# Two-layer hybrid attention kernel: product of a tile's first seven heads one step ahead in the last head of layer 1, four PSUM pairs in the projections of layer 0

## The chip, the cores and the metric

The kernel runs on one NeuronCore of a Trainium2 chip. The metric is device time in microseconds; lower is better. Engines are written as in the profile: PE (TensorE, matmuls), DVE (VectorE), ACT (ScalarE), POOL (GpSimd), SP (its queue issues most DMAs). PSUM, into which PE writes, has 8 banks of 128 x 512 float32; a "pair" here is two banks used as one 128 x 1024 tile.

## The reference

Two layers over 1024 latent tokens of width 1024 and 256 context tokens. Layer 0 is multi-head latent attention (16 heads), layer 1 differential attention (8 heads of two maps each). Each is gated by SiLU, multiplied by the output weights, added to the scaled residual and layer-normalised.

```python
def mla_mixer(h, h_c, rows, need_ctx, w_in, g_qa, w_qb, g_kva, w_kvb):   # layer 0
    q_lat, kv_lat, k_pe, gate = jnp.split(t @ w_in, splits, axis=-1)
    q = (rms_norm(q_lat, g_qa) @ w_qb).reshape(bsz, n, A_HEADS, A_NOPE + A_ROPE)
    kv = (rms_norm(kv_lat, g_kva) @ w_kvb).reshape(bsz, n, A_HEADS, A_NOPE + A_V)
...
    o, o_c = prefix_attention(q, k, v, q_c, k_c, v_c, (A_NOPE + A_ROPE) ** -0.5, need_ctx)
...
def diff_mixer(...):                                                      # layer 1
    q, k, v, gate = jnp.split(t @ w_in, 4, axis=-1)
...
    def combine(o1, o2, gate):
        o = o1 - lam_full.astype(o1.dtype) * o2
        o = rms_norm(o, g_sub) * (1.0 - lambda_init)
        return gated(o, gate)
...
        x = layer_norm(DEEPNORM_ALPHA * x + gate[:, None, :] * (o @ out_w[i]), ln_g[i], ln_b[i])
```

## The kernel before

Tokens are worked on in tiles of 128. A product of float32 accuracy is three matmuls (`mm3`, lines 184 to 187): both operands are split into a high and a low part, and low times low is left out. PE issues in the order of the program text (`manual_schedule`); in the projections at the start of layer 0's attention DVE does too. The other engines' orders are made by a scheduler at build time, which takes what it thinks ready, earlier text first. A PSUM pool (`set_banks`) has so many slots per tag; a new tile takes any slot of its tag that is free, and PE waits if none is.

**Layer 0's start (lines 613 to 883).** The pool has three pairs (tag a) and two single banks (tag d, for the products with V). The list at line 881 orders the work: `pq` and `pq2` make Q and its rotary part, `pk` makes K, each `vg` is one token tile of V (six matmuls of 512 columns into a pair), each `pm` is a piece of the row maxima of head 0 (`max0`: four tiles, the context columns with the maximum `ng`, then its transposition and the write of the maxima into four rows of `qH`). After it come the scores of head 0 (line 833). A V tile is scaled to float16 by ACT (line 650); its low part is made by ACT and POOL for even tiles (lines 653, 654), by DVE for odd ones (line 656). `ab1_of` and `h1_range` (lines 537 to 565) work out a bound for layer 1's input; they run beside head 0.

**The seam between the layers (lines 1145 to 1188).** Layer 0's output product of the tiles 0 to 7 goes by halves, y0 in a bank of tag a, y1 in the one bank of tag b. Then the pool becomes eight single banks of tag b, one is taken and dropped (line 1181), and the first product of layer 1, `made[0]`, starts; after it tile 7 is transposed (`z_turn`), for which its normalisation must be done.

**Layer 1's last head (lines 1569 to 1636).** Layer 1 goes head by head, and in a head tile by tile: a step (`step1`) for a tile t is

- S, the scores (`scores1`): one bank for the context columns of both maps, then two banks for map 0 and two for map 1. DVE takes the maximum of each bank; after map 0's three it makes the bound, and ACT can take the exponentials, which release the banks.
- V, the values (`values1`) of tile t-2, 30 matmuls into one bank; they follow S at once where the budget `at[0]` is 0, as it is in the last head (`SLOTO`).
- T, the transposes (`turn1`) of tile t-1's probabilities, in three pieces, and between them side work, dealt out by a budget of 7000 a slot.

In the last head (h = 7) the side work is the output product. A tile's attention of heads 0 to 6 is loaded (`out_load`), multiplied on POOL by its gate `g` (line 1479) and transposed (`out_turn`, line 1491); head 7 follows when V of the tile is done. `out_tile1(t)` then takes two banks, multiplies heads 0 to 6 for both halves, then head 7 (16 times three matmuls in all), adds the residual, and normalises. It runs in step t+2, so that the steps 0 and 1 have no side work and two steps (8 and 9) follow the last S. The last head's gate column is made at the end of head 6: ACT's SiLU (line 1327), a write to memory (line 1328), and from there `g` is read, two tiles at a time (lines 1458, 1478). Four of the eight blocks of output weights are split in `out_open` (lines 1464 to 1469), ahead of the last head.

Of the kernel before, what the change touches and what calls it, by code (L numbers as in the profile page):

```python
# [17 lines left out]
P = 128  # L18
# [35 lines left out]
def hybrid_kernel(  # L54
# [23 lines left out]
    def set_banks(**tags):  # L78
        pstack.close()
        banks.clear()  # L80
        banks.update(tags)
        banks["pool"] = pstack.enter_context(
            tc.tile_pool(name=nm("psum"), bufs=1, space=bass.MemoryType.PSUM, reuse_waits="tile"))
# [526 lines left out]
            pass  # L610
    p0.close()

    set_banks(a=3, d=2)
    a0 = ctx.enter_context(ExitStack())
    wk = a0.enter_context(spool("a0work"))
    Vh = wk.tile([P, NT, H0, V0 + 1], F16, name="Vh")
# [23 lines left out]
    def prod_v0():  # L640
        pool.memset(Vh[:, :, :, V0:V0 + 1], 1.0)
        for t in range(NT):
            ts = slice(t * P, (t + 1) * P)
            ps = pair()
            for hh in range(2):
                c = slice(hh * 512, hh * 512 + 512)
                mm3(ps[:, c], latH[:, 2, ts], latL[:, 2, ts], wv[0][:, c], wv[1][:, c], True, True)
            src = ps.rearrange("p (h d) -> p h d", d=V0)
            vh = Vh[:, t, :, :V0]
            act.activation(vh, src, AF.Copy, scale=vsc0)  # L650
            if t % 2 == 0:
                vf = w0("op").rearrange("p a b -> p (a b)")[:, :1024].rearrange("p (h d) -> p h d", d=V0)
                act.activation(vf, src, AF.Copy, scale=vsc0)
                pool.tensor_tensor(Vl[:, t, :, :], vf, vh, op=ALU.subtract)
            else:
                dve.scalar_tensor_tensor(Vl[:, t, :, :], src, vsc0, vh, op0=ALU.mult, op1=ALU.subtract)
            yield
# [221 lines left out]
    pm = max0(0, 0)  # L879
    with tc.manual_schedule(engines={ET.PE, ET.DVE}):  # L880
        for g in (pq, pk, pq, vg, pq, pq, vg, pk, pk, pq, pq1, vg, pq2, pq2, pq2, vg,
                  pm, vg, pm, vg, pm, vg, pm, vg, pm, vg, pm, vg):
            next(g)
    ow_ctx = ExitStack()

    def first(g, n):
# [18 lines left out]
    for h in range(H0):  # L905
        last = h == H0 - 1
        even, quad = (h + 1) % 2 == 0, (h + 1) % 4 == 0
        if h == H0 - 2:
            rp.close()
            ow = ow_ctx.enter_context(spool("o0w", side="right"))  # L910
            oH = ow.tile([P, KT, D], F32R, name="oH0")
            oL = ow.tile([P, KT, D], F32R, name="oL0")
            lw = load_outw(oH, oL, lambda: w0("ows"))
        if last:
            run_step(units0(h, 0) + units0(h, 2), [(max0(h, 2), (1, 0, 1)), (max0(h, 1), (0, 1, 1, 1, 2, 1)),
                                                   (lw, (1, 0, 1))])
            octx = {t: (w0(b_), w0(a_))[::-1] for t, a_, b_ in ((8, "rsw", "rr"), (9, "cs", "cs"))}

            def load_ctx():
                yield  # L920
                yield
                for t in (8, 9):
                    for x, d_ in zip(octx[t], (o_d[0], sg_d[0])):
                        sp.dma_start(x, d_[t * P:(t + 1) * P, :])
                    dve.tensor_tensor(*[octx[t][0]] * 2, octx[t][1], op=ALU.mult)
                yield

            run_step(units0(h, 1), [(load_ctx(), (1, 1, 1))])
            tv = lambda x: x.bitcast(F32R).rearrange("p (a b) -> p a b", a=KT)
            tctx = {8: (tv(w0("ows")), tv(w0("ows"))), 9: (tv(w0("rr")), tv(w0("cs")))}  # L930
            with tc.manual_schedule(engines={ENG[c] for c in MAN}):
                def turn_ctx(t):
                    tb = pair()
                    turn_out(octx[t][0], *tctx[t], [tb[:, :512], tb[:, 512:]])

                turn_ctx(8)
                retire(0)
                retire(1)
                for t in (8, 9):
                    y_ = pair()  # L940
                    yctx[t] = [y_[:, :512], y_[:, 512:] if t == 8 else bank("d")]
                    for hh in range(2):
                        c = slice(hh * 512, hh * 512 + 512)
                        mm_out(yctx[t][hh], *tctx[t], c)
                        if t == 8 and hh == 0:
                            turn_ctx(9)
                        flush()
        else:
            kq = chain(prod_k(h + 1), prod_q(h + 1, 0))
            low = [[(first(lw, 3), p_)] if h == H0 - 2 else [] for p_ in ((1, 0, 1, 0, 1), (1, 0, 1, 0, 1))]  # L950
            if h == 0:
                ab1_of()
            hr = [(h1_range(pair), (0, 1, 0, 1, 1))] if h == 0 else []
            run_step(units0(h, 0), hr + [(max0(h, 1), (1, 1, 2, 1, 1)), (max0(h, 2), (0, 1, 0, 1)),
                                    (kq, (2, 2, 1 + quad, 0, 0) if even else (2,))] + low[0])
            qs = chain(prod_q(h + 1, 1), prod_q(h + 1, 2))
            run_step(units0(h, 1) + units0(h, 2), [(max0(h + 1, 0), (1, 1, 1, 2, 1)),
                                                   (qs, (1, 1 + quad, 0, 1) if even else (2,))] + low[1])
# [16 lines left out]
    def w1(tag):  # L975
        sh, d, b = TAG1[tag]
        return rot(place[tag], sh, d, tag, b)
# [70 lines left out]
    with ow_ctx, spool("o0") as op0:  # L1048
# [94 lines left out]
        late = {0: (lam_,), 1: (lam_,), 2: (pw[0],), 3: (pw[0],), 4: (pw[0],), 6: (pw[1],), 7: (pw[1],)}  # L1143
        squares = {0: pw[0], 5: pw[1]}
        for t in range(8):
            y1, y0 = bank("b"), bank("a")
            mm_out(y0, *tHL[t], halves[0])
            if t:
                z_keep(t - 1)
# [28 lines left out]
                next(pw[1])  # L1178
        z_keep(7)
        set_banks(b=8)  # L1180
        bank("b")
        kcols, qcols = slice(P, 2 * P), slice(0, P)
        made = {0: [*proj1(512, 0, kcols)][-1]}
        z_turn(7, [bank("b"), bank("b")])
# [268 lines left out]
    def out_open():  # L1453

        prv.close()
        wg1 = a1.enter_context(spool("a1outg"))
        place["g"] = wg1
        TAG1["g"] = ([P, D], F32, 2)
        og["gb2"] = w1("wsq")
        bcast_row(og["gb2"], ln_g[1:2, :])  # L1460
        rest = [big.tile([P, 5, D], F32R, tag=tg, name=nm("o1")) for tg in ("bigA", "bigB")]
        oHL.extend([r[:, k - NOW, :] for r in rest] for k in range(NOW, KT))
        out_load(0)
        for k, w in enumerate(pre):
            if k % 2:
                split(*oHL[NOW + k], w, e_lo=pool)
            else:
                act.activation(oHL[NOW + k][0], w, AF.Copy, scale=gsub)
                dve.scalar_tensor_tensor(oHL[NOW + k][1], w, gsub, fv(oHL[NOW + k][0]), op0=ALU.mult, op1=ALU.subtract)
            if k == 0:  # L1470
                out_load(1)

    def out_load(t):

# [25 lines left out]
        out_turn(t, 4, 3)  # L1500
        yield 768

    def out_tile1(t):

        ts = slice(t * P, (t + 1) * P)
        tH, tL = oT[t]
        res = w1("res")
        sp.dma_start(res, zn_d[ts, :])
        y = [bank("b") for _ in range(2)]

        def mm(hh, k):
            c = slice(hh * 512, hh * 512 + 512)
            mm3(y[hh], tH[:, k, :], tL[:, k, :], oHL[k][0][:, c], oHL[k][1][:, c], k == 0, k == KT - 1)

        for hh in range(2):
            for k in range(KT - 1):
                mm(hh, k)
                yield 1600
                if hh == 1 and k == 3:
                    out_turn(t, KT - 1, 1)  # L1520
                    yield 256
        z, bs = w1("z"), w1("bs")
        for hh in range(2):
            mm(hh, KT - 1)
            c = slice(hh * 512, hh * 512 + 512)
            dve.tensor_tensor(z[:, c], y[hh], res[:, c], op=ALU.add)
            dve.bn_stats(bs[:, hh, :], z[:, c])
        yield 3200
        mv = w1("mv")
        dve.bn_aggr(mv[:, 0:2], bs)  # L1530
        rstd_of(mv[:, 2:3], mv[:, 1:2], 1.0, 1)
# [11 lines left out]
        pool.tensor_tensor(z, z, og["gb3"], op=ALU.add)  # L1543
        sp.dma_start(out[ts, :], z)
        yield 0

    credit = [0]

# [10 lines left out]
    with tc.manual_schedule(engines={ENG[c] for c in MAN1}):  # L1559
# [47 lines left out]
        for h in range(H1):  # L1607
# [9 lines left out]
            for t in range(SEQ // P):  # L1617
                if last:
                    if t >= 2:
                        out_load(t)  # L1620
                    G = weave(out_tile1(t - 2), out_turns(t - 1), (9, 12)) if t >= 2 else iter(())
                    if t == 2:
                        G = chain(out_turns(0), G)
                    credit[0] = 0
                step1((h, t), G, SLOT1 if not last else SLOTO)
                if last:
                    for _ in G:
                        pass
            for _ in G:
                pass  # L1630
        for t in range(SEQ // P - 2, SEQ // P):
            G = weave(out_tile1(t), out_turns(t + 1), (9, 12))
            credit[0] = 0
            step1(None, G, SLOTO)
            for _ in G:
                pass
# [74 lines left out]
```

## Time and profile before

| what | us |
|---|---|
| median of 3 runs (lowest, highest) | 1792.3 (1790.97, 1795.45) |
| the profiled execution's own time | 1792.78 |
| its span in the trace | 1790.9 |
| around the span | 1.88 |
| projections at the start of layer 0's attention | 223 to 259 of the span |
| seam of the layers (first product of layer 1) | 907 |
| last head of layer 1 | 1628 to 1791 |

Times in rows are counted from the start of the span. A timeline row has the start, the duration, the engine, the line of the kernel, the operation, output <- inputs, the shape, and in square brackets the idle time of the engine just before it and what ended it. A matmul's duration covers its run through the array; matmuls are issued closer together than that. A row of the windows has the busy time of each engine (with the number of instructions), then PE's mean granted clock as a share of full speed, then the share of DMA.

### The profile page before, as it was taken

The page shows a single profiled execution, that of the slowest core. Times are in us where ns is not written, and L with a number is a line of the kernel's source. Part 1 is how long each engine was busy: PE and PEld are TensorE (multiplying, and loading weights), DVE is VectorE, ACT ScalarE, POOL GpSimd, SP SyncE. Part 2 cuts the span into 40 slices and gives each one's busy share as a digit, 9 for nine tenths or more (in the row PEclk, how much of TensorE's full clock was granted, in tenths as well). Part 3 has the DMA queues.
Part 4 walks back from the last instruction along what each step waited for, and adds up shares of the span by engine and source line. Part 5 has one row for each costly group of instructions (what it writes and reads, how often), then busy time and mean ns, then how long its engine had stood idle before and what let it go on. Part 6 is the DMA issues. An engine that isn't in the chain of part 4 may idle for free. (4 is left out here: it accounts for less than half of the span.)

```text
span 1790.9 us, 36759 instructions
## 1 busy us (share of the span) xinstructions
PE 1664.6 (93%) x14564; PEld 1232.2 (69%) x14564; DVE 1228.9 (69%) x2045; ACT 1119.1 (62%) x2235; POOL 797.3 (45%) x724
## 2 busy tenths in 40 slices
PE   7999989999999998999999999999999999987998
PEld 6999955666666665577866666767675767566776
DVE  7658666575665666647855777777877787877664
ACT  2551167877777777845535676767676676757542
POOL 1432136767767776746551222231313131454454
PEclk9999999999999999999999999999999999998999
DMA  8358520110110122155532213131212122232331
GB/s 299 86 148 256 166 63 23 38 47 24 42 46 24 39 56 69 56 195 174 167 109 61 79 54 79 54 80 54 64 39 63 41 60 63 61 125 67 103 114 71
DMA packets 111226, 154.84 MB, mean 86 GB/s; under 512 B 13416, under 2 KB 84680, under 8 KB 111055
## 3 DMA queue, kind: packets, MB, share of 16 engines
q1 hardware_dynamic: 102654, 144.90, 27.2%
q10 hardware_dynamic: 8400, 7.61, 1.3%
q8 instruction: 114, 1.87, 0.5%
q14 instruction: 58, 0.47, 0.1%
HBM read 98.65 MB, written 27.07 MB: 70 GB/s over the span
## 5 line engine op out<-in xcount | busy, mean ns | idle before, releaser
L779 POOL TENSOR_TENSOR pl<-p,ph 128x1024 f16<-128x1024 f32 (+1 forms) x176 | 364.6, 2077 | 150.4 <-ACT ph L778 123.7
L1365 ACT ACTIVATE p<-ps_b,mx 128x512 f32<-128x512 f32 (+1 forms) x384 | 230.4, 617 | 85.0 <-DVE mx L1361 83.4
L777 ACT ACTIVATE p<-ps_a,esc 128x1024 f32<-128x1024 f32 (+1 forms) x176 | 189.0, 1074 | 94.5 <-PE ps_a L835 88.6
L759 DVE TENSOR_REDUCE mx<-ps_a 128x1 f32<-128x1024 f32 x128 | 155.2, 1222 | 128.3 <-PE ps_a L757 128.3
L778 ACT CAST ph<-p 128x1024 f16<-128x1024 f32 (+1 forms) x176 | 177.1, 1006 | 5.5
L1359 DVE TENSOR_REDUCE mx<-ps_b 128x1 f32<-128x512 f32 x256 | 165.5, 680 | 1.5 <-PE ps_b L1343 1.4
L848 PE MATMUL ps_d<-Vh,pl 128*128 128x65 f16 x1344 | 146.0, 194 | 4.5 <-POOL pl L779 4.4
L845 PE MATMUL ps_d<-Vh,ph 128*128 128x65 f16 x1344 | 148.1, 195 | 0.0
L847 PE MATMUL ps_d<-Vl,ph 128*128 128x64 f16 x1344 | 146.9, 193 | 0.0
L1342 PE MATMUL ps_b<-KS,QS 128*128 128x512 f16 (+1 forms) x384 | 127.9, 350 | 10.7 <-DVE pl L182 5.0
L845 PEld LDWEIGHTS <-ph 128*128 128x128 f16 x1344 | 123.2, 97 | 18.0 <-issue 4.6
L847 PEld LDWEIGHTS <-ph 128*128 128x128 f16 x1344 | 123.9, 98 | 12.1
L1378 PE MATMUL ps_b<-idr,p 128*128 128x128 f32 x640 | 103.4, 277 | 30.3 <-ACT p L1365 15.4
L1343 PE MATMUL ps_b<-KS,Q 128*128 128x512 f16 (+1 forms) x384 | 130.8, 349 | 0.0
L833 PE MATMUL ps_a<-qH,KH 100*128 100x512 f16 x320 | 121.8, 381 | 8.6 <-ACT p L777 4.2
L1390 POOL TENSOR_TENSOR sm<-sm,us 128x1 f32<-128x1 f32 x64 | 15.7, 246 | 255.0 <-DVE sm L1369 251.0
L848 PEld LDWEIGHTS <-pl 128*128 128x128 f16 x1344 | 123.1, 97 | 5.8 <-POOL pl L779 5.8
L182 DVE SCALAR_TENSOR_TENSOR pl<-ps_b,lcf,ph 128x512 f16<-128x512 f32 (+1 forms) x192 | 117.0, 654 | 13.0 <-ACT ph L181 13.0
L181 ACT ACTIVATE ph<-ps_b,lcf 128x512 f16<-128x512 f32 (+1 forms) x192 | 114.9, 646 | 17.0 <-PE ps_b L1378 17.0
L834 PE MATMUL ps_a<-qH,KL 96*128 96x512 f16 x320 | 121.6, 380 | 0.0
L835 PE MATMUL ps_a<-qL,KH 96*128 96x512 f16 x320 | 120.9, 378 | 0.0
L1378 PEld LDWEIGHTS ps_b<-idr,p 128*128 128x128 f32 x640 | 77.5, 142 | 56.5 <-ACT p L1365 23.7
(428 smaller groups left out, 5276.1 us busy)
## 6 DMA issues: line engine op xcount, KB each, us to landing
ws<-in_dw SPq DMA_DIRECT2D x28, 512.0 KB, 3.9
adw<-in_ada_w SPq DMA_DIRECT2D x24, 512.0 KB, 4.7
adaw<-in_ada_w SPq DMA_DIRECT2D x16, 512.0 KB, 7.7
g<-sg_d SPq DMA_DIRECT2D x16, 512.0 KB, 8.8
sg_d<-gg ACTq DMA_DIRECT2D x40, 128.0 KB, 3.7
o_d<-op SPq DMA_DIRECT2D x7, 640.0 KB, 4.0
xt<-in_xT SPq DMA_DIRECT2D x16, 256.0 KB, 3.8
wgs<-in_w_in SPq DMA_DIRECT2D x32, 128.0 KB, 3.1
```

Source lines behind the costliest of these rows:

```text
L759: dve.tensor_reduce(mx[:, t, 0:1], ps, axis=AX.X, op=ALU.max)
L777: act.activation(p32[:, :n], st, AF.Exp, scale=esc0)
L778: act.copy(ph[:, :n], p32[:, :n])
L779: pool.tensor_tensor(pl[:, :n], p32[:, :n], ph[:, :n], op=ALU.subtract)
L845: pe.matmul(pv[:, t, :], ph[:, ts], Vh[:, k, h, :], start=(k == kcs[0] and t == 0), stop=False, skip_group_check=True)
L847: pe.matmul(pv[:, t, :V0], ph[:, ts], Vl[:, k, h, :], start=False, stop=False, skip_group_check=True)
L848: pe.matmul(pv[:, t, :], pl[:, ts], Vh[:, k, h, :], start=False, stop=(k == NT - 1), skip_group_check=True)
L1342: pe.matmul(out, qs[m][:, ts], ks[m][:, c0:c0 + n], start=True, stop=False)
L1343: pe.matmul(out, q1[m][:, ts], ks[m][:, c0:c0 + n], start=False, stop=True)
L1359: dve.tensor_reduce(mx[:, 2 + 2 * m + i:3 + 2 * m + i], b, axis=AX.X, op=ALU.max, negate=True)
L1365: act.activation(p[m][:, c0:c0 + n], b, AF.Exp, bias=nb, accum_out=sm[:, 2 + 3 * m + i:3 + 3 * m + i])
L1378: pe.transpose(st[:, j * P:(j + 1) * P], pc[:, (k0 + j) * P:(k0 + j + 1) * P], idn)
```

## The change

In layer 0's start the pool has four pairs and no single banks; it goes back to three pairs and two banks after the list. Of the last six `pm` and `vg` the order is changed, and the V tiles whose low part goes by ACT and POOL are 1, 3, 5, 7 and 8 (still five of ten). `ab1_of` and `h1_range` run beside head 2. At the seam, tile 7's y1 goes into the bank of tag e, and no bank is dropped. In the last head of layer 1 the pool has five banks of tag b and three of a new tag y for the products; `g` has three buffers. A tile's heads 0 to 6 are multiplied one step earlier, in step t+1, of tile 0 half of them in step 0; head 7, the sum and the normalisation stay in step t+2. The splitting of the four weight blocks is dealt out over step 0.

```diff
-    set_banks(a=3, d=2)
+    set_banks(a=4)
...
-            if t % 2 == 0:
+            if t in (1, 3, 5, 7, 8):
...
-                  pm, vg, pm, vg, pm, vg, pm, vg, pm, vg, pm, vg):
+                  pm, vg, pm, vg, pm, vg, pm, pm, vg, vg, pm, vg):
             next(g)
+    set_banks(a=3, d=2)
...
-            if h == 0:
+            if h == 2:
                 ab1_of()
-            hr = [(h1_range(pair), (0, 1, 0, 1, 1))] if h == 0 else []
+            hr = [(h1_range(pair), (0, 1, 0, 1, 1))] if h == 2 else []
...
-            y1, y0 = bank("b"), bank("a")
+            y1, y0 = bank("b" if t < 7 else "e"), bank("a")
...
         set_banks(b=8)
-        bank("b")
...
-        TAG1["g"] = ([P, D], F32, 2)
+        TAG1["g"] = ([P, D], F32, 3)
...
+        set_banks(b=5, y=3)
         out_load(0)
+        out_load(1)
+
+    def out_split():
+
         for k, w in enumerate(pre):
...
-            if k == 0:
-                out_load(1)
+            yield 0
...
-    def out_tile1(t):
...
+    def out_mm(t, hh, k):
+
+        if k == 0:
+            oy[t, hh] = bank("y")
         tH, tL = oT[t]
...
+        c = slice(hh * 512, hh * 512 + 512)
+        mm3(oy[t, hh], tH[:, k, :], tL[:, k, :], oHL[k][0][:, c], oHL[k][1][:, c], k == 0, k == KT - 1)
+
+    def out_heads(t, hh, ks):
+        for k in ks:
+            out_mm(t, hh, k)
+            yield 1600
+
+    def out_last(t):
+
+        z, bs, res = w1("z"), w1("bs"), ores.pop(t)
+        for hh in range(2):
+            out_mm(t, hh, KT - 1)
             c = slice(hh * 512, hh * 512 + 512)
...
+            dve.tensor_tensor(z[:, c], oy[t, hh], res[:, c], op=ALU.add)
             dve.bn_stats(bs[:, hh, :], z[:, c])
         yield 3200
...
+    def out_step(s):
+
+        if s == 0:
+            yield from weave(chain(out_turns(0), *[out_heads(0, hh, range(NOW)) for hh in range(2)]), out_split(),
+                             (3, 5, 7, 9))
+            return
+        prev, opened = s - 2, s - 1
+        heads = range(NOW if s == 1 else 0, KT - 1)
+        if prev >= 0:
+            ores[prev] = w1("res")
+            sp.dma_start(ores[prev], zn_d[prev * P:(prev + 1) * P, :])
+        if opened < SEQ // P:
+            yield from out_heads(opened, 0, heads[:-2])
+        if prev >= 0:
+            out_turn(prev, KT - 1, 1)
+            yield 256
+        if opened < SEQ // P:
+            yield from out_heads(opened, 0, heads[-2:])
+        end = out_last(prev) if prev >= 0 else iter(())
+        yield from (v for _, v in zip(range(1), end))
+        yield from out_turns(s)
+        yield from end
+        if opened < SEQ // P:
+            yield from out_heads(opened, 1, heads)
...
-                    G = weave(out_tile1(t - 2), out_turns(t - 1), (9, 12)) if t >= 2 else iter(())
-                    if t == 2:
-                        G = chain(out_turns(0), G)
+                    G = out_step(t)
...
-        for t in range(SEQ // P - 2, SEQ // P):
-            G = weave(out_tile1(t), out_turns(t + 1), (9, 12))
+        for t in range(SEQ // P, SEQ // P + 2):
+            G = out_step(t)
```

More of the change, by code (lines that the diff above doesn't have):

```diff
@@ L1501, in out_turns @@
         yield 768
-    def out_tile1(t):
-        ts = slice(t * P, (t + 1) * P)
+    oy, ores = {}, {}
+    def out_mm(t, hh, k):
+        if k == 0:
+            oy[t, hh] = bank("y")
         tH, tL = oT[t]
[L1507 to L1511, printed above, removed]
-            c = slice(hh * 512, hh * 512 + 512)
[L1513 to L1526, printed above, removed]
+        c = slice(hh * 512, hh * 512 + 512)
[8 more added lines that the diff above has]
+            out_mm(t, hh, KT - 1)
+            c = slice(hh * 512, hh * 512 + 512)
+            dve.tensor_tensor(z[:, c], oy[t, hh], res[:, c], op=ALU.add)
             dve.bn_stats(bs[:, hh, :], z[:, c])
         yield 3200
+        ts = slice(t * P, (t + 1) * P)
         mv = w1("mv")
```

## The prediction

> **What bounds the kernel now.** First the span, then the last head's stretch by stages, then who PE waited for there. PE's last matmul starts at 1781.98 and issues in 0.23, so the stretch is cut at 1782.21; 1632.00 is the end of V of tile 6, head 6. Columns: bounds, length, busy time of PE, of its weight loads, DVE, ACT, POOL, PE's granted clock, DMA.
>
> ```profile
> span 1790.9 us, 36759 instructions
> 1632.00:1656.24 24.24, 14.70 (x114) 9.58 (x111) 20.07 (x33) 19.11 (x47) 14.38 (x13) 0.79 0.34 115
> 1656.24:1782.21 125.97, 125.85 (x781) 100.71 (x781) 75.25 (x152) 57.26 (x144) 60.17 (x63) 1.00 0.31 98
> PE ps_b L1378 <- DVE pl L182: 5.8, 1, 5.8
> PE ps_b L1378 <- DVE p L1371: 3.1, 1, 3.1
> 1686.74 0.28 PE L1342 MATMUL ps_b<-KS,QS 128*128 128x256 f16 x1
> 1691.34 0.40 PE L185 MATMUL ps_b<-oH,wx 128*128 128x512 f32 x1
> 1692.03 0.40 PE L185 MATMUL ps_b<-oH,wx 128*128 128x512 f32 x1
> 1703.70 0.28 PE L1342 MATMUL ps_b<-KS,QS 128*128 128x256 f16 x1
> 1704.04 0.27 PE L1343 MATMUL ps_b<-KS,Q 128*128 128x256 f16 x1
> 1705.87 0.22 PE L1386 MATMUL ps_b<-vh,ph 128*128 128x128 f16 x1
> 1781.98 0.39 PE L187 MATMUL ps_b<-o,wy 128*128 128x512 f32 x1
> ```
>
> From step 2's products on (1656.24) PE is the bound: 125.85 busy of 125.97 at full clock, a step each 16.96 (1703.70 - 1686.74). S takes 2.17 of it (to 1705.87), a head's three matmuls 0.69 (1692.03 - 1691.34). Only ahead of that is PE idle, 24.24 - 14.70 = 9.5, and it works there at a lowered clock. The first wait is for a bank: S of the last head held five of eight, V one, T two, and T's third piece waited 5.8 until DVE freed one. The second is for data.
>
> So filling the steps 0 and 1 can win no more than 9.5 and the lost clock. That is at most 0.21 x 24.24 = 5.1; in proportion to PE's work (14.70 of 24.24) I take 3.1. The work that PE has from 1632.00 to its end, at full clock, is then 150.2 - 9.5 - 3.1 = 137.6, and the change removes none of it.
>
> **The last head, step 0.** PE now meets tile 0's transposes right behind V of (6,6), and everything of PE stands behind them: T of (6,7), then step 1. They need tile 0 multiplied by a gate that comes out of the head before.
>
> ```profile
> 1628.47 1.17 ACT L1468 ACTIVATE o<-z,gsub 128x1024 fp32r<-128x1024 f32 x1
> 1632.54 1.15 ACT L1327 ACTIVATE gg<-gg,uw 128x1024 f32<-128x1024 f32 x1
> 1633.72 0.37 SPq L1328 DMA_DIRECT2D sg_d<-gg  x1
> 1637.50 0.85 SPq L1478 DMA_DIRECT2D g<-sg_d  x2
> 1642.14 4.12 POOL L1479 TENSOR_TENSOR ws<-ws,g 128x896 f32<-128x896 f32 x2 [1.81 <-DMA g<-sg_d]
> ```
>
> Here the gate is done at 1633.69, written from 1633.72, read from 1637.50, there at 1642.14, and tile 0 is multiplied by 1642.14 + 4.12/2 = 1644.2. The change takes the weight splitting (1.17 on ACT) out of the way, up to 1.1 earlier: 1643.1. SP no longer has a load of `res` ahead of the read, and fewer loads share the queues; if that halves the 3.8 between write and read, 1641.2, and 1640.3 with a quicker landing. I take 1641.8. Until then PE idles (V of (6,6) itself waits for one of five banks, inside this time).
>
> From 1641.8 the 137.6 follow, with four additions.
>
> **A bank for V in the steps 1 to 7.** S takes all five banks, and V, next in PE's order, needs the first that an exponential frees.
>
> ```profile
> 1620.09 0.68 DVE L1355 TENSOR_REDUCE mx<-ps_b 128x2 f32<-128x512 f32 x1
> 1622.32 0.69 ACT L1365 ACTIVATE p<-ps_b,mx 128x512 f32<-128x512 f32 x1 [3.19 <-DVE mx L1361]
> 1692.68 0.67 ACT L1365 ACTIVATE p<-ps_b,mx 128x512 f32<-128x512 f32 x1
> ```
>
> The context scores are in PSUM 0.61 after S begins (1704.04 + 0.27 - 1703.70); from DVE's first maximum to the end of the first exponential it is 2.92 (1620.09 to 1623.01), here with DVE and ACT waiting for nothing else. That is 3.53 against S's 2.17: a wait of 1.36, seven times, 9.5. The other end is the steady step of now, where ACT takes the previous tile's normalisation first and the first exponential ends at 1693.35, 6.61 after S began at 1686.74: 4.4 a step, 31 in all. The change moves that normalisation into the middle of the step, so I take the low figure; nothing below 0 is possible, and 0 is a rival.
>
> **The clock after idling, and the first split.** What idling costs is shown at the start of layer 0, and what a shorter wait costs beside head 0.
>
> ```profile
> 235.33 0.50 PE L185 MATMUL ps_a<-wvH,latH 128*128 128x512 f32 x1 [2.04 <-DVE stqL L182]
> 236.00:241.00 5.00, 4.73 (x21) 3.75 (x20) 2.33 (x4) 3.59 (x6) 1.20 (x1) 0.66 0.46 109
> 273.84 0.22 PE L768 MATMUL ps_a<-idr,ng 128*4 128x128 f32 x1 [1.44 <-DVE hm L300]
> 275.82 0.38 PE L833 MATMUL ps_a<-qH,KH 100*128 100x512 f16 x1 [1.38 <-DVE qH L769]
> 271.00:276.00 5.00, 2.17 (x31) 1.41 (x30) 4.57 (x18) 2.50 (x3) 3.67 (x2) 1.00 0.15 39
> ```
>
> After 2.04 of idling PE loses 0.34 x 5.0 = 1.7; waits of 1.44 and 1.38 in one stretch left it at 1.00. So step 0's wait costs 1.7 more, and the seven waits of 1.36 none. The transposes' copy to SBUF adds 0.6 (the row of ACT below).
>
> **The tail.** Before, V of tile 7 is followed by 42 matmuls of heads 0 to 6 that hide the way to head 7. After the change these stand ahead of V, and PE waits.
>
> ```profile
> 1771.01 0.22 PE L1388 MATMUL ps_b<-vh,pl 128*128 128x128 f16 x1
> 1771.88 0.19 ACT L1392 ACTIVATION_READ_ACCUMULATOR o<-o 128x1 f32 x1
> 1773.06 0.19 POOL L159 TENSOR_SCALAR ss<-ss 128x1 f32<-128x1 f32 x1
> 1773.92 0.35 DVE L1397 SCALAR_TENSOR_TENSOR ws<-o,ss,g 128x128 f32<-128x128 f32 x1 [2.22 <-POOL ss L160]
> 1778.65 0.27 PE L1491 MATMUL ps_b<-idr,ws 128*128 128x128 f32 x1
> 1778.96 0.27 ACT L176 CAST wx<-ps_b 128x128 fp32r<-128x128 f32 x1 [4.70 <-PE ps_b L1491]
> ```
>
> V to the accumulator's end 1.06 (1771.01 to 1772.07), POOL to the end of the scaling 1.21 (1773.06 to 1774.27), transpose to the end of its copy 0.58 (1778.65 to 1779.23): 2.9. The last six matmuls, 1.38 at full clock, then run at half, 1.3 more: 4.2. POOL's normalisation of tile 6 may stand in between: up to 6.
>
> Sum: 1641.8 + 137.6 + 9.5 + 1.7 + 0.6 + 4.2 = 1795.4 against 1782.2: the last head loses **13.2**. What follows the last matmul stays.
>
> **Layer 0's start.** PE takes 35.60 there, with these waits beside the 2.04 shown.
>
> ```profile
> 223.06:258.66 35.60, 28.70 (x121) 20.57 (x119) 23.24 (x22) 21.39 (x23) 12.34 (x7) 0.92 0.31 82
> PE ps_a L757 <- DVE Vl L656: 1.4, 2, 0.7
> PE ps_a L185 <- DVE mx L759: 1.1, 2, 0.5
> 256.25 0.22 PE L768 MATMUL ps_a<-idr,ng 128*4 128x128 f32 x1 [2.12 <-DVE ng L765]
> 231.03 3.06 DVE L295 TENSOR_TENSOR rr<-rr,rsw 128x1024 f32<-128x1024 f32 x1
> 230.93 2.07 POOL L654 TENSOR_TENSOR Vl<-op,Vh 128x1024 f16<-128x1024 f32 x1 [5.58 <-ACT op L653]
> ```
>
> All but the 2.12 are waits for a pair; a fourth covers them, and two V tiles (twelve matmuls of 0.23) now stand ahead of the transposition that waited 2.12. Waits together 6.7, lost clock 0.08 x 35.6 = 2.8: at most 9.5. DVE's sum of 3.06 ran beside POOL's subtraction and ended 1.1 after it; with tile 0 on DVE (its 1.28 of line 656 takes POOL's place) the two don't meet. DVE is busy 23.24 and ACT 21.39 of it whatever the pairs, and the loads of K and Q still come in their order, so I take two thirds, **-6.5**; 0 at worst, since no engine gets more work but DVE 1.28 early and less late.
>
> **Head 2 for head 0, the seam.** The 1.44 and 1.38 above are head 0's wait for the bound's small operations; beside head 2 they come in the same order ahead of the same `ng`: what one head wins the other loses, 0 (from -2 to +1).
>
> ```profile
> 907.15 0.38 PE L185 MATMUL ps_b<-h1H,wx 128*128 128x512 f16 x1 [2.00 <-DVE z L1083]
> 910.12 1.24 ACT L1092 ACTIVATE z<-z,mv 128x1024 f32<-128x1024 f32 x1 [5.88 <-POOL mv L1091]
> ```
>
> `made[0]` waits 2.00 for tile 7's y1 in its bank. With y1 elsewhere it starts at 905.15, and its 24 matmuls (S's 2.17 are eight of that width and four half as wide, so 0.217 each) end at 910.4; `z_turn` then waits for ACT until 911.36. So **-0.9**, between 0 and -2.
>
> **Sum.** The profiled execution took 1792.78 (1.88 around its span), 0.5 above the median: 1792.8 + 13.2 - 6.5 - 0.9 = 1798.6, **1799**.
>
> **The rivals.**
>
> *The bank is there in time* (not slower). If a bank frees within S's own 2.17 the steps lose nothing: 1798.6 - 9.5 = 1789; with all of layer 0's 9.5 won, 1786. It decides from the point where the first exponential ends before S does. Against it stands 2.92 in DVE and ACT alone; for it, that T's 5.8 shows the wait only with eight banks full.
>
> *The fill pays.* If tile 0 is ready by 1637, PE starts 4.8 earlier: 1794. For it: 1.1 of ACT and the `res` load go; against it: the landing took 4.64 (1637.50 to 1642.14) and the product 2.06.
>
> *The clock falls in each step.* The waits for a bank come once in some 18 us; if each cools the clock as 2.04 did, seven times 1.7: 1811. Against it the row with 1.44 at clock 1.00; for it, that DVE or ACT need be only 0.7 late for a wait of 2.04. (The Trainium skill, TensorE: Matmul & The Clock Gate, A second HAM failure mode: psum-queue depth-cycling, describes a kernel in which cycling through PSUM left PE idle so often for moments that its clock swung between half and full. By that rule this is the time; here the rows show it from 2.04 on and not at 1.44.)
>
> *The pairs don't bind.* If DVE and ACT set layer 0's start, nothing is won there: 1805.
>
> **How the numbers follow.** Forecast 0.46, bank in time 0.26, fill 0.11, clock 0.08, pairs 0.09. A measurement here tells 0.3% from no change, 5.4 us: faster is below 1786.9, slower above 1797.7. The forecast's own range is 1793 to 1805, about four fifths of it slower; clock and pairs are slower; the fill is mostly no change; the bank case is half faster, half no change. Slower 0.56, same 0.29, faster 0.15. The range 1786 to 1811 leaves out the far ends (31 for the banks, a last head that gains).
>
> **What would show it.** V's first matmul in each step waiting for ACT's exponential, 1.4 long, with S's period near 18.3; step 0 with a wait of PE at tile 0's transposes until about 1642; a gap of 3 in PE ahead of the last six matmuls; head 0's first scores at about 252 in place of 258.66; `made[0]` without its 2.00. It is wrong if the steps keep 16.96, or if PE's stretch from step 0 on begins well ahead of 1640.

## The result, and the profile after

The change makes the kernel slower: 1821.8 us (median of 4 runs, 1818.3 to 1825.7) against 1791.6 (4 runs, 1788.0 to 1795.5) beside it, a ratio of 1.0166 with a 95% interval of 1.0149 to 1.0184, so about 30 us. The forecast was 1799, with 1811 as the end of the range. The profiled execution of after took 1823.78, with 1821.9 of span.

First the last head of both kernels in one row each, from the first matmul of S of (7,0) to the end of the last matmul (columns as in the forecast's rows of windows). The first fence is before, the second after; after's two other rows start at tile 0's transposes and cover one steady step.

```profile
1628.14:1782.37 154.23, 144.57 (x936) 113.17 (x933) 99.34 (x190) 80.21 (x196) 75.95 (x78) 0.97 0.31 99
```

```profile
span 1821.9 us, 36757 instructions
1623.61:1813.40 189.79, 153.76 (x936) 121.17 (x933) 100.76 (x190) 80.65 (x196) 81.40 (x78) 0.93 0.24 80
1640.43:1813.65 173.22, 147.75 (x892) 116.91 (x892) 88.67 (x173) 66.51 (x169) 74.80 (x73) 0.94 0.21 72
1706.88:1727.10 20.22, 17.32 (x110) 13.55 (x109) 11.72 (x23) 7.55 (x22) 9.71 (x8) 1.00 0.31 101
```

PE issues the same 936 matmuls in both, and the stretch is 35.6 longer. PE's idle time in it goes from 9.7 (154.23 - 144.57) to 36.0, which is 26.4 of the 35.6; the other 9.2 is the same work done at a lower clock (0.93 in place of 0.97). A step takes 20.2 instead of 16.96. The last head began 4.5 earlier (1623.61 for 1628.14): 35.6 - 4.5 is the 31 by which the spans differ.

Next, what PE waited for in the last head of after (the view of waits: total, times, longest), and one steady step in order of time (the first matmul of S, DVE, ACT, then V).

```profile
PE ps_b L1386 <- ACT p L1365: 24.0, 8, 6.3
PE ps_b L1495 <- DVE ws L1397: 7.0, 6, 4.3
PE ps_b L1495 <- POOL ws L1483: 3.8, 1, 3.8
1706.88 0.28 PE L1342 MATMUL ps_b<-KS,QS 128*128 128x256 f16 x1
1707.53 0.69 DVE L1355 TENSOR_REDUCE mx<-ps_b 128x2 f32<-128x512 f32 x1 [2.21 <-PE ps_b L1343]
1708.14 2.48 DVE L1359 TENSOR_REDUCE mx<-ps_b 128x1 f32<-128x512 f32 x4
1710.53 0.45 DVE L1361 TENSOR_SCALAR mx<-mx 128x1 f32<-128x1 f32 x2
1710.83 0.69 ACT L1365 ACTIVATE p<-ps_b,mx 128x512 f32<-128x512 f32 x1 [3.73 <-DVE mx L1361]
1711.66 0.22 PE L1386 MATMUL ps_b<-vh,ph 128*128 128x128 f16 x1 [2.44 <-ACT p L1365]
```

The wait for V's bank is there, at the instruction and behind the engine that the forecast named, eight times (6.3 of it in step 0, 2.4 to 2.8 in the steps 1 to 7). What differs is DVE: it takes all four maxima of line 1359 in one go, map 1's two among them, and only then makes a bound. So the first exponential ends 4.64 after S begins (1711.52 - 1706.88), not 3.53.

The second row of waits is head 7's transposition, which waits for line 1397, the scaling that V's result goes through. The third is tile 0 in step 0: the way of the gate, from the SiLU to the first transposes.

```profile
1628.04 1.15 ACT L1327 ACTIVATE gg<-gg,uw 128x1024 f32<-128x1024 f32 x1
1629.21 0.37 SPq L1328 DMA_DIRECT2D sg_d<-gg  x1
1632.58 0.32 SPq L1560 DMA_DIRECT2D res<-zn_d  x1
1633.00 1.32 SPq L1482 DMA_DIRECT2D g<-sg_d  x3
1637.61 2.77 POOL L1483 TENSOR_TENSOR ws<-ws,g 128x896 f32<-128x896 f32 x1 [5.06 <-DMA g<-sg_d]
1640.43 1.75 PE L1495 MATMUL ps_b<-idr,ws 128*128 128x128 f32 x7 [3.75 <-POOL ws L1483]
```

Nothing on this way got shorter: 3.79 from the write's issue to the read's (3.78 before), 4.61 until the read has landed (4.64 before), a load of `res` still ahead of it on SP (line 1560, which the program text has only in step 2), and the gate itself as long after S began as before (5.58 and 5.55). The product on POOL even took longer: 2.77 where half of before's 4.12 is 2.06.

At the other places: the first scores of head 0 come at 251.29 (258.66 before), the two waits for the bound of layer 1's input now stand beside head 2, as long as they were (1.50 and 1.4 for 1.44 and 1.38), and `made[0]` starts without its wait.

### The profile page after: what moved, and what is told of

The parts are those of the page before. It is cut to its first block, busy times and chain, and to the rows that moved or that the text cites. A ratio compares the mean times of both kernels' runs of the same rounds, so it can differ in the third digit from the quotient of the medians.

```text
span 1821.9 us, 36757 instructions
## 1 busy us (share of the span) xinstructions
PE 1673.5 (92%) x14564; PEld 1239.2 (68%) x14564; DVE 1230.0 (68%) x2045; ACT 1120.0 (61%) x2235; POOL 802.4 (44%) x724
## 5 line engine op out<-in xcount | busy, mean ns | idle before, releaser
L1386 PE MATMUL ps_b<-vh,ph 128*128 128x128 f16 x640 | 115.6, 224 | 24.2 <-ACT p L1365 24.0
```

## The experiments

All runs are medians against the kernel before on the same chip. The last column is the last head from S of (7,0) to the end of the last matmul, from each trace.

| run | what | us | ratio (95%) | last head |
|---|---|---|---|---|
| before | | 1791.6 | 1 | 154.2 |
| after | | 1821.8 | 1.0166 (1.0149 to 1.0184) | 189.8 |
| E1 | layer 0 and seam alone | 1784.7 | 0.9953 (0.9939 to 0.9968) | 152.7 |
| E2 | last head alone | 1825.6 | 1.0187 (1.0171 to 1.0202) | 188.8 |
| E3 | after, V between the maps | 1797.9 | 1.0033 (1.0022 to 1.0045) | 165.8 |
| E4 | after, three heads between the maps | 1826.3 | 1.0186 (1.0170 to 1.0202) | 190.3 |
| E5 | E3, three heads kept for the tail | 1797.0 | 1.0042 (1.0029 to 1.0056) | 166.2 |
| E6 | E3, tile 0 a step later | 1796.3 | 1.0041 (1.0028 to 1.0054) | 163.7 |
| E7 | after, map 0's bound first | 1817.3 | 1.0146 (1.0129 to 1.0162) | 184.0 |
| E8 | before with banks 5 and 3 | 1830.6 | 1.0228 (1.0215 to 1.0241) | 194.3 |
| E9 | before with four pairs | 1791.4 | 1.0003 (0.9992 to 1.0013) | |
| E10 | E1, splits in step 1 | 1787.3 | 0.9980 (0.9970 to 0.9989) | 156.5 |
| E11 | E1, splits in step 0 | 1786.2 | 0.9973 (0.9962 to 0.9985) | 155.6 |
| E12 | E1 with banks 5 and 3, V between the maps | 1804.5 | 1.0071 (1.0054 to 1.0087) | 173.4 |

Profiled executions differ by some us ahead of the last head where the code is the same (it begins at 1619.20 in E3's and at 1625.97 in E6's), so lengths of that stretch are compared, not its place.

**E1 and E2: which half of the change.** E1 has the hunks of the diff for layer 0, for head 2 in place of head 0 and for the seam, with the old last head; E2 has the others, with the old layer 0 and seam.

> The layer 0 edits, head 2 for head 0 and the seam's bank, with the last head as it was before. Theory (the two parts of the change add, and the whole loss lies in the last head): the first scores of head 0 come at about 251.3, the last head starts 4.5 earlier than before (1623.6 for 1628.14) and takes 162.8 as before; time 1787. Rival (the gain of layer 0 is lost again further on, since the last head waits for loads and for the gate that do not move with it): 1790.5 to 1792.

> The last head's edit alone, layer 0 and the seam as before. Theory (the parts add): the last head takes 198 instead of 162.8, time 1791.6 + 30.2 + 4.5 = 1826. Rival (part of the loss comes from the earlier start, which only moves PE's work ahead of data that come when they came): at most 1822.

E1 gains 7.4 (1784.67 against 1792.08, the theory had 1787) and E2 loses 33.5 (1825.63 against 1792.08, as the theory had it). Together that is a loss of 26, against 30 for the whole change; by the intervals of the three ratios the two agree. E2 shows the same row of waits for V's bank, 24.0 in 8 waits, so nothing in it needs the earlier start. E1 is faster than both kernels, and no other version that was run has a lower median.

**E3: V between the maps.**

```diff
                 if cur:
                     S = scores1(*cur)
                     next(S)
             some(side, at[0])
             with tc.high_priority(HP):
+                if at is SLOTO and turned:
+                    values1(*turned.pop(0))
                 if cur:
                     next(S)
-                if turned:
+                if at is not SLOTO and turned:
                     values1(*turned.pop(0))
```

> The changed kernel with V put between the scores of map 0 and of map 1 in the last head, so that V needs no bank that an exponential frees; what waits for such a bank is then the fifth piece of S, behind 3.2 us of V. Theory (the wait for V's bank is what the steps lose, and the clock falls with it): the seven waits of 2.44 (17.7 in all) go and with them most of the clock lost in the steps 1, 2 and 6 (1.7 + 1.6 + 1.7); S's period goes from 20.2 to about 17.3; time 1799 to 1804. Step 0's 6.3 does not count, since tile 0 is awaited there anyway. Rival (the step is set by the way from scores over exponentials, T and its splits to V): PE waits elsewhere in the step as long, time 1815 to 1822.

The theory's step came true, and the time is a little below its 1799: 1797.9. The 3.2 for V in that text is V at about half clock; at full clock it takes 1.6. The profile of E3, waits and one step:

```profile
PE ps_b L1495 <- POOL ws L1483: 9.9, 1, 9.9
PE ps_b L1495 <- DVE ws L1397: 5.1, 2, 4.3
PE ps_b L1342 <- ACT o L1391: 2.2, 1, 2.2
1674.23:1691.42 17.19, 17.06 (x110) 13.61 (x110) 12.01 (x23) 9.22 (x23) 8.79 (x9) 1.00 0.35 120
```

V's row is gone, a step is 17.19 at full clock, and the last head is 24.0 shorter than in after. The waits left are step 0's for tile 0 (9.9; V of (6,6), which stood in this wait, is done earlier now) and the tail's 4.3.

**E4: the same cover, taken from behind V.**

```diff
-                step1((h, t), G, SLOT1 if not last else SLOTO)
+                step1((h, t), G, SLOT1 if not last else (4800 if t else 0, *SLOTO[1:]))
```

> The changed kernel with three heads' products of the open tile (nine matmuls, 2.07) put between the scores of map 0 and of map 1 in the steps 1 to 7. Theory (as for V between the maps): DVE has only map 0's maxima at hand, so its bound comes 1.2 earlier; the first exponential ends about 3.6 after S begins, V stands at 4.24: no wait, S's period about 17.3, time 1799 to 1804. Rival (the way from scores to T sets the step; map 1's scores now come 2.07 later, and so does everything behind them): 1810 to 1822, with PE waiting at T or at the next V for the splits.

Neither: V's wait all but goes, and the time doesn't fall. The waits of E4 (7.1 of the second row stands in step 0):

```profile
PE ps_b L1495 <- DVE ws L1397: 23.8, 7, 4.3
PE ps_b L1386 <- ACT p L1365: 9.8, 4, 7.1
```

The three heads' products that now stand ahead of V are missing behind it, where in after five heads' products covered the way from V over ACT, POOL and DVE to head 7's transposition. That wait was 7.0 in after; here it is 23.8, some 3.3 in each steady step (13.1 in four between 1680 and 1770). Work can cover one of two waits, and in after the second was only just covered.

**E5 and E6: what is left of E3.** E5 keeps three heads' products of tile 7 for the last step; E6 moves tile 0's transposes and its first products out of step 0.

```diff
+        if s == SEQ // P + 1:
+            yield from out_heads(prev, 1, range(KT - 4, KT - 1))
         if prev >= 0:
             out_turn(prev, KT - 1, 1)
...
-            yield from out_heads(opened, 1, heads)
+            yield from out_heads(opened, 1, range(KT - 4) if s == SEQ // P else heads)
```

```diff
-            yield from weave(chain(out_turns(0), *[out_heads(0, hh, range(NOW)) for hh in range(2)]), out_split(),
-                             (3, 5, 7, 9))
+            yield from out_split()
             return
...
-        heads = range(NOW if s == 1 else 0, KT - 1)
+        heads = range(KT - 1)
+        if s == 1:
+            yield from out_turns(0)
```

> V between the maps as in the run before, and of tile 7 the last three heads' products of the second half (nine matmuls, 2.07) kept for the last step, behind V of tile 7. Theory (the 4.3 of the tail is the uncovered way from V over ACT, POOL and DVE to head 7's transposition): that wait falls from 4.3 to about 2.3 and the last matmuls run at a higher clock; 1797.9 - 2.1 to - 3.4, so 1794.5 to 1796. Rival (the three heads are missed in step 8, where V of tile 7 then waits for T's splits): 1797 to 1799.

> V between the maps, and tile 0's transposes with its first four heads' products moved from step 0 to step 1, behind S of (7,1) and V of (6,7); the splits of the last weights stay in step 0. Theory (PE waits 9.9 at tile 0's transposes for the gate's way through DRAM, with everything behind them): T of (6,7), S and V of step 1 (2.2 + 3.2, T about 2) run inside that wait; the wait falls by 5 to 7.3, time 1790.6 to 1793. Rival (S of (7,1) has to wait for the banks that the exponentials of (7,0) free, and these come late in step 0): 1796 to 1798.

Both come out at the times of their rivals, and by the intervals neither differs from E3 in time. The rows of E5, then of E6:

```profile
PE ps_b L1495 <- DVE ws L1397: 3.7, 2, 2.9
PE ps_b L1386 <- ACT ph L181: 0.9, 1, 0.9
```

```profile
1636.62 0.58 PE L1342 MATMUL ps_b<-KS,QS 128*128 128x512 f16 x1 [5.98 <-ACT p L1365]
```

In E5 the tail's wait falls from 4.3 to 2.9 and V of tile 7 now waits 0.9 for T's split, as the rival said; the last head is no shorter (166.2 and 165.8). In E6 the 9.9 is gone, but the fifth piece of S of (7,0) itself waits 5.98 for a bank that an exponential of (7,0) holds; S of (7,1), which the rival named, starts behind that, at 1640.41, without such a wait. ACT starts that exponential only at 1635.79, behind the gate's SiLU and four casts of weights. So step 0 can't work ahead of its own exponentials with five banks, and the last head is only 2.1 shorter.

**E7: map 0's bound ahead of map 1's maxima.** The bound's instruction writes two columns more, which map 1's maxima overwrite, so DVE can't take those first.

```diff
+            if h == H1 - 1 and m == 0:
+                dve.tensor_scalar(mx[:, 4:7], mx[:, 0:3], mx[:, 3:4], mx[:, 0:1], op0=ALU.min, op1=ALU.min)
+            else:
-            dve.tensor_scalar(nb, mx[:, 2 * m + 2:2 * m + 3], mx[:, 2 * m + 3:2 * m + 4], mx[:, m:m + 1],
+                dve.tensor_scalar(nb, mx[:, 2 * m + 2:2 * m + 3], mx[:, 2 * m + 3:2 * m + 4], mx[:, m:m + 1],
```

> The changed kernel, but map 0's bound writes two more columns that map 1's maxima overwrite, so that DVE must take it ahead of them; the same number of instructions. Theory (the forecast's 1.36 was right for map 0's maxima alone, and the other 1.1 is map 1's two maxima of 0.6 taken ahead of the bound): V's wait falls from 2.44 to about 1.3 in each of seven steps, S's period from 20.2 to about 19.0; 1821.8 - 8 = 1814, and 1808 to 1810 if waits so short leave the clock at 1.00. Rival (the first exponential is held by ACT or by PE, not by DVE's order): 1820 to 1823.

The profile of E7 (its lines 1362, 1368 and 1389 are the bound, the exponential and V): one step, V's waits between 1660 and 1770, then the waits of the whole last head.

```profile
1706.33 1.28 DVE L1359 TENSOR_REDUCE mx<-ps_b 128x1 f32<-128x512 f32 x2
1707.65 0.32 DVE L1362 TENSOR_SCALAR mx<-mx 128x3 f32<-128x3 f32 x1
1708.00 0.69 ACT L1368 ACTIVATE p<-ps_b,mx 128x512 f32<-128x512 f32 x1 [2.49 <-DVE mx L1362]
PE ps_b L1389 <- ACT p L1368: 9.5, 6, 2.3
...
PE ps_b L1389 <- ACT p L1368: 18.0, 8, 6.3
PE ps_b L1498 <- DVE ws L1400: 8.1, 7, 4.3
```

The four maxima fall apart into two and two, and the exponential follows the first pair. The waits for V's bank lose 6.0 (24.0 to 18.0), the last head 5.8. Without the longest, which is step 2's, the waits between 1660 and 1770 are 1.4 each ((9.5 - 2.3) / 5), where the theory said 1.3; the steps 1 and 2 still wait 2.3. The median falls by 4.5 where the theory had 8 or more, and as the intervals of E7 and after overlap, it is the trace and not the time that shows the step. In the steps 3 to 7 DVE's order is the difference between 1.4 and 2.4 of wait.

**E8 and E12: the banks without the move.** E8 is the kernel before with `set_banks(b=5, y=3)` in the last head and `y` taken from the three; E12 is that on E1, with E3's order of V and the maps.

```diff
+        set_banks(b=5, y=3)
...
-        y = [bank("b") for _ in range(2)]
+        y = [bank("y") for _ in range(2)]
```

> The kernel before with five banks for S, V and T and three for the products in the last head, and nothing moved: layer 0 as before. Theory (the fewer banks make V wait for an exponential, whatever stands ahead; here ACT takes the previous tile's normalisation first, and the first exponential ends 6.61 after S begins against S's 2.17): V waits about 4.4 in each of the steps 1 to 7, the time rises by some 25 to 31, 1817 to 1823. Rival (the loss needs the moved products: with the old order DVE and ACT are relieved elsewhere and V waits no more than 1): 1792 to 1800.

> The layer 0 and seam edits (1784.7), the old last head's order with five banks for S, V and T and three for the products, and V put between the scores of map 0 and of map 1. Theory (five banks cost only through V's wait, and what the changed order still loses with V between, 1797.9 against 1784.7, lies in step 0's wait for tile 0 and in the tail, which the old order does not have): V's wait goes, the fifth piece of S waits at most about 1 a step because ACT takes the previous tile's normalisation ahead of the first exponential; 1785 to 1792. Rival (five banks cost also at T and at the fifth piece, whatever the order): 1797 or more, with S's period at 18.5 or above against 16.96.

E8 is the slowest of all, 39.5 above before with nothing moved, more than the theory's 25 to 31. E12 comes out as its rival: 1804.5, 19.8 above E1, with S's period at 19.1 to 20.7. E8's waits, two of its steps and two rows of the second of them, then E12's waits and two rows of ACT:

```profile
PE ps_b L1386 <- ACT p L1365: 31.3, 8, 7.2
1676.80:1699.20 22.40, 18.68 (x110) 14.86 (x109) 12.56 (x24) 8.77 (x22) 9.95 (x9) 0.92 0.28 92
1699.20:1722.50 23.30, 19.58 (x110) 15.64 (x108) 12.55 (x24) 8.77 (x22) 9.92 (x9) 0.85 0.27 88
1699.87 1.28 DVE L1528 BATCH_NORM_STATS2 bs<-z 128x6 f32<-128x512 f32 x2
1704.31 0.67 ACT L1365 ACTIVATE p<-ps_b,mx 128x512 f32<-128x512 f32 x1
```

```profile
PE ps_b L1342 <- ACT o L1391: 10.3, 5, 2.1
1710.46 1.24 ACT L1542 ACTIVATE z<-z,mv 128x1024 f32<-128x1024 f32 x1 [5.48 <-POOL mv L1541]
1711.61 0.35 ACT L1391 ACTIVATE o<-ps_b,sm 128x128 f32<-128x128 f32 x1
```

In E8 V waits 31.3 in all, 7.2 of it in step 0 and 24.1 in the steps 1 to 7, and where the wait is 3.7 the clock falls too: steps of 22.4 and 23.3. That the 31.3 meets the 31 of the forecast's other end is chance, since that was seven times 4.4 without step 0; by the step it is 3.4. More stands on the way than the forecast named: DVE takes the previous tile's statistics (1.28) ahead of the maxima, and ACT its normalisation ahead of the exponential, which ends 5.92 after S began at 1699.06. In E12 V doesn't wait, but the fifth piece of S does, 2.1 in each of the steps 3 to 7, for the bank that V's result leaves, since ACT waits for that same normalisation and does it (1.24) ahead of the copy. So in the old order the divided banks cost much wherever V stands, and the moved order, with the normalisation out of ACT's way, bears them better: E3 is 6.6 below E12, with the same layer 0. The moved order with eight banks in common was not run, so what it would gain without the division is open.

**E9: the four pairs alone.**

```diff
-    set_banks(a=3, d=2)
+    set_banks(a=4)
...
             next(g)
+    set_banks(a=3, d=2)
```

> The kernel before with four pairs instead of three in layer 0's start, and nothing else: its old list of turns, V's tiles split between POOL and DVE as before, head 0 and the last head as before. Theory (the three waits for a pair, 2.04 + 1.4 + 1.1, and the clock that fell with them, are most of the gain): head 0's first scores at 253 to 255 in place of 258.66, the wait of 2.12 at the transposition stays; 1791.5 less 4 to 5.5, 1786 to 1788. Rival (the gain comes from DVE's tile 0 and from the two V tiles ahead of the transposition, the pairs bind little): 1790 to 1792.

No gain: 1.0003, with an interval from 0.9992 to 1.0013. The rows of E9:

```profile
251.73 0.22 PE L768 MATMUL ps_a<-idr,ng 128*4 128x128 f32 x1 [2.12 <-DVE ng L765]
256.71 0.58 PE L833 MATMUL ps_a<-qH,KH 100*128 100x512 f16 x1 [2.52 <-DVE Vl L656]
```

The transposition of the maxima comes 4.5 earlier than before (256.25), so the pairs do bind. But then the first scores wait 2.52 for DVE's subtraction of the last V tile, whose pair belongs to the pool that closes there; they come only 2.0 earlier, and nothing of that is left at the end. In E1 the V tiles' new places and their new division between the engines take this wait away. Which of the two does more was not tried alone.

**E10 and E11: splits of the weights later, on E1.** `out_open`'s splits become a generator of their own (as in the change), run in step 1 or in step 0.

```diff
+                    if t == 1:
+                        G = out_split()
```

> The layer 0 and seam edits with the old last head (1784.7), and the splits of the last four weights taken from ahead of the last head into step 1. Theory (in step 0 four casts of 4.3 in all on ACT and two differences of 1.3 and 2.1 on DVE stand ahead of the first exponential of (7,0), and PE then waits 5.8 and 2.6): the first exponential comes up to 4 earlier and those waits shrink by 3 to 5: 1780 to 1782. Rival (ACT and DVE have as much to do in step 1, and the products of heads 4 to 7 of tile 0 in step 2 wait for the splits): 1785 to 1789.

> The same with the splits in step 0, as the changed kernel has them, behind S and V there. Theory (only what stands ahead of the first exponential counts, so anywhere behind S is early enough): 1780 to 1783. Rival (with the planner's order ACT still takes the splits ahead of the exponentials, as in the changed kernel's step 0): 1784 to 1786.

No gain in either: the last heads are 3.8 and 2.9 longer than E1's. The waits of E10 and three rows of its step 0, then the waits of E11:

```profile
PE ps_b L1378 <- DVE pl L182: 5.8, 1, 5.8
PE ps_b L1388 <- DVE pl L182: 2.9, 1, 2.9
1629.32 2.05 DVE L1473 SCALAR_TENSOR_TENSOR o<-z,gsub,o 128x1024 fp32r<-128x1024 f32 x1
1629.95 1.03 ACT L176 CAST o<-res 128x1024 fp32r<-128x1024 f32 x1
1632.30 0.69 ACT L1365 ACTIVATE p<-ps_b,mx 128x512 f32<-128x512 f32 x1
```

```profile
PE ps_b L1378 <- ACT p L1365: 5.5, 1, 5.5
```

The edits moved the splits in the program text only. In both runs the scheduler still has ACT take all four casts ahead of the first exponential of (7,0), as in E1; the second difference of DVE and the last cast of E10 are in its rows, and behind that difference DVE comes at once to the split that frees the bank for T's third piece. So the wait of that piece stays (5.8 and 5.5), and whether the splits hold it is not tested by these runs. E11's rival named this order. In E10 V of step 2 waits 2.9 that it did not wait before.

## Why the prediction was wrong, and where it was right

The sign, the place and the mechanism were right; the sum of the last head, 13.2, was far too small for the 35.5 to the end of the span. By the forecast's own terms, of which the bank for V and the clock missed most, 8.2 and 6.4 of 22.8:

| term | forecast | measured |
|---|---|---|
| S of (7,0) to tile 0's transposes | 13.7 | 16.8 |
| PE's work from there at full clock | 137.6 | 138.4 |
| V's bank, steps 1 to 7 | 9.5 | 17.7 |
| head 7's way, first split and other waits | 3.5 | 7.8 |
| clock from there on | 3.0 | 9.4 |

The 17.7 is 24.0 less step 0's 6.3; all idle time from the transposes on is 25.5 (173.22 - 147.75). The clock's 9.4 comes from the stretches of after in which it stood below 1.00, and the work is what remains of 147.75:

```profile
1640.43:1650.65 10.22, 10.19 (x41) 8.18 (x42) 1.91 (x3) 1.77 (x4) 7.92 (x7) 0.73 0.17 59
1650.65:1666.40 15.75, 12.95 (x87) 10.24 (x85) 8.98 (x17) 8.22 (x22) 2.41 (x4) 0.89 0.01 4
1666.40:1686.70 20.30, 17.50 (x103) 14.06 (x102) 12.48 (x25) 8.41 (x22) 5.00 (x7) 0.92 0.25 75
1747.30:1768.35 21.05, 18.61 (x109) 14.96 (x108) 11.74 (x23) 8.90 (x23) 9.50 (x9) 0.92 0.30 97
1800.00:1813.70 13.70, 8.71 (x55) 6.33 (x53) 2.98 (x8) 2.64 (x6) 6.44 (x7) 0.88 0.09 38
```

The length of each times what its clock lacks of 1.00 is 2.8, 1.7, 1.6, 1.7 and 1.6. Step 0's cold start, three steps and the tail are seen here. It is an estimate: in the steps 2 and 6 some 0.5 of it fell while PE waited anyway.

- **The bank for V: right mechanism, wrong size.** The step that failed is "from DVE's first maximum to the end of the first exponential it is 2.92", taken from one step of head 6, where twelve matmuls of side work (1619.27 to 1620.58) stand between the scores of the two maps, so that DVE met map 0's maxima first. That the last head's S, with nothing between, puts map 1's maxima at hand before the bound, and that DVE's order isn't the text's, was not weighed: the first exponential ended 4.64 after S began, not 3.53. E7 shows the 1.36 itself to be right: with map 0's bound first the steps 3 to 7 wait 1.4.
- **The clock: the wrong case was called the likely one.** "... the seven waits of 1.36 none" holds for 1.36 (E7's steps of 1.4 to 1.6 between 1686 and 1763 ran at 1.00), but the waits were 2.4 to 2.8, and in three of the seven steps (1, 2 and 6) V ran at half clock. The rival put that at 1.7 a step, which is what each cost; it came in three. (The Trainium skill, TensorE: Matmul & The Clock Gate, A second HAM failure mode: psum-queue depth-cycling, describes such swinging; the trace agrees for three steps of seven.)
- **Step 0.** That the change "takes the weight splitting (1.17 on ACT) out of the way" and the halved 3.8 both failed: ACT still did a cast of line 1473 (1.17, at 1623.97) ahead of the gate's SiLU and two more casts behind it, ahead of the exponentials; SP still had a `res` load ahead of the read, and the landing took as long as before. The orders of ACT and SP are the scheduler's, not the text's. The fill rival fell with them.
- **The tail.** From V's last matmul to the end of the transposition's copy it took 5.28 (1805.20 to 1810.48) instead of 2.9, of which PE waited 4.34 and 0.35: POOL's normalisation of tile 6 stood in between until 1808.3, which the forecast named as possible and did not count. The steps themselves added 2.7 of the same wait that the forecast had at nothing; E4 shows how thin its cover was.
- **Layer 0 and the seam: right.** -6.5 and -0.9 forecast (two thirds of 9.5 is 6.3), 7.4 measured together in E1. In the profile the scores of head 0 come 7.4 earlier. At the seam the way from the last matmul of tile 7's product to its transposes takes 6.65 (899.29 to 905.94) in place of 7.58 (904.75 to 912.33), 0.9 less as forecast: `made[0]` loses its 2.00, and the transposes then wait 1.06 for ACT. The rival that the pairs don't bind is wrong as a cause (E9's transposition moves by 4.5), though the pairs alone gain nothing.
- **Head 2 for head 0: right.** The same waits of 1.5 and 1.4, now beside head 2.

The range missed because its upper end came from one rival at a time. Higher waits and the lower clock are one case: waits of 1.4 to 1.6 left the clock at 1.00 in E7, and of those of 2.4 to 2.8 in after three of seven lowered it. The far end that the range left out, 31 for the banks, would have given 1798.6 + 31 - 9.5 = 1820, next to the measured 1821.8; that would have been luck, as the waits of the steps 1 to 7 came to 17.7, and the step by which it was reckoned, ACT's normalisation ahead of the exponential, isn't in after.

## What to carry to other kernels

Taking banks out of a common pool has a price of its own, and it can be tried alone: E8 with five and three banks and no other edit lost more than the whole change. Before an order is changed to cover a wait, list what stands behind the work that is moved: E4 won V's wait (24.0 to 9.8) and lost as much at the next one (7.0 to 23.8). A line moved in the text may move nothing on an engine whose order a scheduler makes (E10, E11); look in the trace whether it moved. And if a time rests on the order in which a scheduled engine takes its instructions, work out the sum for the other order too.

## What the hardware showed that was not expected

A wait of the same length leaves PE's clock alone in one step and halves it in another. Two V's of after, each with its first and its last matmul (30 in all):

```profile
1711.66 0.22 PE L1386 MATMUL ps_b<-vh,ph 128*128 128x128 f16 x1 [2.44 <-ACT p L1365]
1713.27 0.22 PE L1388 MATMUL ps_b<-vh,pl 128*128 128x128 f16 x1
...
1752.07 0.27 PE L1386 MATMUL ps_b<-vh,ph 128*128 128x128 f16 x1 [2.44 <-ACT p L1365]
1755.11 0.26 PE L1388 MATMUL ps_b<-vh,pl 128*128 128x128 f16 x1
```

Both waited 2.44; the first V takes 1.61 from first to last issue, the second 3.04. Of the five waits of 2.44 in after one halved the clock, and both of 2.75; in E12 a wait of 2.06 in each step left the clock at 0.92 in three of four steps between 1664.9 and 1746.2, and at 1.00 in the other. (The Trainium skill, TensorE: Matmul & The Clock Gate, What's actually happening, says that the gate watches PE's activity in windows of about 3.4 us that run freely, so that the point of a change depends on where in the window the first matmul lands. The trace doesn't show the windows; it agrees as far as equal pauses end differently. That the clock falls after an idle window of about 3.4, which the same section gives, is not what these rows show, where 2.44 was enough.)

The 2.7 of short waits at head 7's transposition have a neighbour that wasn't expected either. In the four steps of after in which that wait is 0.46 to 0.49, POOL's small operation on V's result (line 159, 128 x 1) takes 1.47, beginning 0.13 behind DVE's combination of the two maps (line 1371, 1.55 long) and ending with it; in the steady steps of before, where the two don't meet, it takes 0.19. No run kept them apart, so that this makes the waits is not shown.
